# Masked decays on ScalarE for wide float32r products, and group-norm steps on VectorE, in the two mixers of a diffusion block

## Chip, cores and metric

One core of a Trainium2 chip runs the whole program. The metric is device time in microseconds, the median of several executions; lower is better. Engine names are those of the profile: PE (TensorE), PEld (its weight loads), DVE (VectorE), ACT (ScalarE), POOL (GpSimd), SP (SyncE, which issues most DMAs).

## What is computed

Two layers, each of them FFN, mixer, FFN, on 512 latent and 256 context tokens of width 1024, all in float32. The mixer projects the tokens and runs four groups of 256 channels side by side: windowed attention, a bidirectional state-space scan (SSD), grouped-query attention and neighbourhood attention. Each group's output is normalised by its root mean square, and one output projection merges the four. The change touches the SSD group:

```python
def ssd_chunked(x, dt, A, Bh, Ch, h0):
    ...
    cum = jnp.cumsum(dtc * A, axis=2)
    seg = cum[:, :, :, None, :] - cum[:, :, None, :, :]
    lmat = jnp.exp(jnp.where(tril, seg, -jnp.inf))
    att = jnp.einsum('bcihn,bcjhn->bcijh', Cc, Bc) * lmat * dtc[:, :, None]
    y = jnp.einsum('bcijh,bcjhp->bcihp', att, xc)
    ...
    y = y + jnp.einsum('bcihn,bchpn,bcih->bcihp', Cc, jnp.moveaxis(h_start, 0, 1), jnp.exp(cum))
```

The chunk is 128 tokens, there are four heads and two directions, and the last line of `merge_groups` that matters here is `yf * lax.rsqrt(jnp.mean(yf * yf, -1, keepdims=True) + EPS)`, times a gain, per group.

## The kernel before

**Products.** Wide products use float32r: each operand is split into a rounded high part (a cast by ACT, for weights L328) and a low rest (a subtraction by DVE, L329), and `mm3` (L335 to L337) issues three matmuls, high by high, high by low and low by high. Other matmuls have plain float32 operands; the trace shows each of those as two instructions (16 rows for 8 matmuls at L1299).

**Order.** A scheduler orders each engine's instructions when the program is built, from the order in which the code emits them. The mixer interleaves generators: `side_by_side(self.ssd(...), n, projections, 10)` runs the SSD scan beside the projections for the windowed and the grouped-query attention, whose matmuls fill PE while the scan waits for ACT and DVE. Within an engine, instructions run strictly in the order so fixed.

**The scan.** `ssd` makes `dtA` (time step times decay rate, 128 positions by 6 chunks by 8, that is two directions of four heads), then the chunk states, and then calls `chunk_out(t)` per chunk of 128 tokens: chunks 4, 5 (context) and 0 to 3 in layer 0, chunks 0 to 3 in layer 1, ten in all. Per chunk:

- POOL writes two tiles `ld0` and `ld1` of 128x512 (L1294): dtA, spread along the free axis, times the strict triangle GT or LT, for four heads. Each has one buffer, so the next chunk's tiles wait for this chunk's readers.
- PE makes the segment sums `seg` (L1299): per head and direction one 128x128 product with ld as the stationary operand and the triangle U or L as the moving one, eight in all; ACT takes their exponential (`segE`, L1301).
- PE multiplies B by C (`G`, L1304), DVE masks the result (`gm`, L1310) and multiplies it by segE in place and into `att` (L1312), and PE adds up `yd` from both (L1319).
- For the carried state PE makes the cumulative decay in `two[:, 0]` (L1330): per direction, pair and head one 128x128 product, with dtA spread over 64 columns as the stationary operand; and the state's product in `two[:, 1]` (L1332). ACT takes the exponential (`ec`, L1336), and DVE combines all into `zs`.

Chunks 4 and 5 have one direction in the last step, the others two.

**The group norm.** `finish_ssd` calls `group_chunk` for two halves of the channels: ACT squares, POOL multiplies by the gain (L1160), PE sums. `end_group` has DVE compute the reciprocal root, POOL spread it on a diagonal (L1175), PE broadcast it and DVE scale. `place_group` splits the result for the output projection: ACT casts (L1188), POOL subtracts (L1189). These steps run beside the windowed attention.

Other POOL work in the mixers, which stays there: the rotary tables of the grouped-query projections (L862, L866) and the issue of the neighbourhood bias loads (L978 to L981).

Of the kernel before, what the change touches and what calls it, by code (L numbers as in the profile page):

```python
# [11 lines left out]
F32 = mybir.dt.float32  # L12
F32R = mybir.dt.float32r
I32 = mybir.dt.int32
AF = mybir.ActivationFunctionType
ALU = mybir.AluOpType
# [3 lines left out]
P = 128  # L20
# [71 lines left out]
def bcast(ap, n):  # L92

    s = list(ap.shape)
    return ap.unsqueeze(len(s)).to_broadcast(s + [n])


def bcast1(ap, n):

    s = list(ap.shape)  # L100
    return ap.unsqueeze(1).to_broadcast([s[0], n] + s[1:])
# [27 lines left out]
class Block:  # L129
# [1023 lines left out]
    def group_chunk(self, l, group, i, o, y, last, tmp):  # L1153

        nc = self.nc
        nt = 4 if last else 6
        n = nt * P
        sq = self.sb(tmp, [NT], "P", bufs=3)[:, :n]
        nc.scalar.square(sq, o[:, :n])
        nc.gpsimd.tensor_scalar(y[:, i, :n], o[:, :n], self.normT[:, l, 2 * group + i:2 * group + i + 1], None,  # L1160
                                op0=ALU.mult)
        ps = self.ps1()
        for t in range(nt):
            nc.tensor.matmul(ps[:, t:t + 1], lhsT=sq[:, t * P:(t + 1) * P], rhs=self.ones[:, 0:1], start=True, stop=True)
        nc.vector.tensor_copy(self.gss[:, 6 * i:6 * i + nt], ps[:, :nt])

    def end_group(self, y, last, tmp):

        nc = self.nc
        nt = 4 if last else 6  # L1170
        ss = self.sb(tmp, [6], "mss", bufs=2)[:, :nt]
        nc.vector.tensor_tensor(ss, self.gss[:, :nt], self.gss[:, 6:6 + nt], op=ALU.add)
        r = self.rsqrt(tmp, ss, nt, 1.0 / 256)
        dg = self.sb(tmp, [NT], "P", bufs=3).rearrange("p (t c) -> p t c", c=P)[:, :nt]
        nc.gpsimd.tensor_tensor(dg, bcast1(self.ident, nt), bcast(r, P), op=ALU.mult)  # L1175
        for lo, hi in ((0, NX), (NX, NT))[:1 if last else 2]:
            ps = self.ps1()[:, :hi - lo]
            nc.tensor.matmul(ps, lhsT=self.ones, rhs=dg[:, lo // P:hi // P].rearrange("p t c -> p (t c)"),
                             start=True, stop=True)
            for i in range(2):  # L1180
                nc.vector.tensor_tensor(y[:, i, lo:hi], y[:, i, lo:hi], ps, op=ALU.mult)

    def place_group(self, group, y, last):

        n = NX if last else NT
        for i in range(2):
            h, lo = self.act[0][:, 2 * group + i, :n], self.act[1][:, 2 * group + i, :n]
            self.nc.scalar.copy(h, y[:, i, :n])  # L1188
            self.nc.gpsimd.tensor_tensor(lo, y[:, i, :n], h.bitcast(F32), op=ALU.subtract)  # L1189


    def softplus(self, x, tmp):
# [19 lines left out]
    def ssd(self, l, last, tmp):  # L1212
        nc = self.nc
        U, L, GT, LT = (self.cst[:, k:k + P] for k in (K_U, K_L, K_GT, K_LT))
# [3 lines left out]
        self.softplus(dtf, tmp)  # L1218
        dtA = self.sb(tmp, [6, 8], "dtA")
        nc.vector.tensor_tensor(dtA, dt, bcast1(self.A[:, l], 6), op=ALU.mult)  # L1220
        ps = self.ps1()
        for d, m in ((0, GT), (1, LT)):
            nc.tensor.matmul(ps[:, 24 * d:24 * d + 24].rearrange("p (t e) -> p t e", t=6), lhsT=m,
                             rhs=dtA[:, :, 4 * d:4 * d + 4], start=True, stop=True)
# [55 lines left out]
        for t in (3, 2, 1):  # L1280
            v = lambda x: x[:, 1].rearrange("p (h c) -> p h c", h=4)
            x = self.sb(tmp, [256], "ychunk")
            nc.vector.tensor_tensor(x.rearrange("p (h c) -> p h c", h=4), v(state[t]), bcast(dec[:, t, 4:8], 64),
                                    op=ALU.mult)
            nc.vector.tensor_tensor(state[t - 1][:, 1], state[t - 1][:, 1], x, op=ALU.add)

        def chunk_out(t):
            q = col(t)
            first = {4: (1,), 5: (0,)}.get(t, (0, 1))

            ld = []
            for d, m in ((0, GT), (1, LT)):
                x = self.sb(tmp, [4, P], f"ld{d}", bufs=1)
                nc.gpsimd.tensor_tensor(x, bcast(dtA[:, t, 4 * d:4 * d + 4], P), bcast1(m, 4), op=ALU.mult)  # L1294
                ld.append(x)
            seg = self.ps1()
            for h in range(4):
                for d, m in ((0, U), (1, L)):
                    nc.tensor.matmul(seg[:, h * P:(h + 1) * P], lhsT=ld[d][:, h], rhs=m, start=d == 0, stop=d == 1)  # L1299
            E = self.sb(tmp, [2, 2, P], "segE", bufs=1)  # L1300
            nc.scalar.activation(E.rearrange("p g r c -> p (g r c)"), seg, AF.Exp)  # L1301
            G = self.ps1()
            for g in range(2):
                nc.tensor.matmul(G[:, g * P:(g + 1) * P], lhsT=uT[:, 2 + g, q:q + P], rhs=uT[:, 4 + g, q:q + P],  # L1304
                                 start=True, stop=True)
# [10 lines left out]
            for pr in range(2):  # L1316
                for d in range(2):
                    for a in range(2):
                        nc.tensor.matmul(yd[64 * a:64 * a + 64, pr * P:(pr + 1) * P], lhsT=xd[:, d, 2 * pr + a],  # L1319
                                         rhs=att[d][:, pr, a], start=d == 0, stop=d == 1)  # L1320

            two = self.ps2()
            for d, m in ((0, U), (1, L)):
                if d not in first:
                    continue
                for pr in range(2):
                    at = (2 * d + pr) * P
                    for a in range(2):
                        e = 4 * d + 2 * pr + a
                        nc.tensor.matmul(two[64 * a:64 * a + 64, 0, at:at + P],  # L1330
                                         lhsT=dtA[:, t, e:e + 1].to_broadcast([P, 64]), rhs=m, start=True, stop=True)
                    nc.tensor.matmul(two[:, 1, at:at + P], lhsT=state[t][:, d, pr * P:(pr + 1) * P],  # L1332
                                     rhs=uT[:, 4 + pr, q:q + P], start=True, stop=True)
            lo, hi = 256 * first[0], 256 * first[-1] + 256
# [224 lines left out]
```

## Time and profile before

| What | Value |
| --- | --- |
| Median of 3 runs | 2965.39 us (2965.01 to 2967.98) |
| Profiled execution, its own time | 2970.67 us |
| Span in its trace | 2968.9 us |
| Mean granted PE clock | 0.988 of 2.4 GHz |
| Scan and its projections, layer 0 | about 655 to 820 us, chunk outputs from 715 |
| Scan and its projections, layer 1 | about 2250 to 2372 us, chunk outputs from 2305 |
| Windowed attention with the group norm | about 820 to 895 us and 2372 to 2430 us |

The page names what is busy; what counts is what PE waits for in each stage, since an engine that is off the path may idle or work without cost. In the timeline a matmul's start-to-start distance is its price: the durations beside it contain the pipeline's length and overlap.

### The profile page before, as it was taken

What the parts mean: (1) busy time and instruction counts of PE and PEld (TensorE: products, weight loads), DVE (VectorE), ACT (ScalarE), POOL (GpSimd) and SP (SyncE); (2) the same over time, 40 slices, a digit from 0 to 9 for tenths busy, and PEclk for the clock granted to TensorE, in tenths of its full rate; (3) what the DMA queues carried; (4) which work ended last, traced back from release to release, by engine and by line L of the source; (5) the groups of instructions that cost most, each with busy time, mean ns of one, the idle gap of its engine ahead of it and who ended that gap; (6) DMA issues with size and microseconds to landing.
All of it is one profiled execution on the core that took longest, in us unless ns stands there. A gap on an engine that the chain in (4) does not pass through costs nothing.

```text
span 2968.9 us, 43652 instructions
## 1 busy us (share of the span) xinstructions
PE 2867.3 (97%) x16412; PEld 2451.8 (83%) x16412; DVE 2068.6 (70%) x4258; ACT 1149.6 (39%) x2103; POOL 494.2 (17%) x372
## 2 busy tenths in 40 slices
PE   7999999999999998999999999999999999899997
PEld 4898888888787777888878789999988787788886
DVE  4766668775758787666577976766886757776558
ACT  4333233352256543322324433333344256443333
POOL 1222122100110002221211122221200110012112
PEclk9999999999999999999999999999999999999998
DMA  6443334231124223534435122212132143242332
GB/s 230 144 162 107 121 100 141 77 100 49 29 78 83 94 72 104 178 122 141 157 103 168 57 67 75 76 58 74 56 97 72 44 110 89 78 125 86 95 100 72
DMA packets 319207, 296.09 MB, mean 100 GB/s; under 512 B 16311, under 2 KB 244751, under 8 KB 318739
## 3 DMA queue, kind: packets, MB, share of 16 engines
q1 hardware_dynamic: 317939, 290.80, 31.6%
q0 software_dynamic: 1056, 2.49, 0.4%
q8 instruction: 130, 2.13, 0.3%
q14 instruction: 82, 0.67, 0.1%
HBM read 270.52 MB, written 7.39 MB: 94 GB/s over the span
## 4 chain that ended last, share of the span: by engine, by line
PE 77%; DVE 15%; issue 3%; ACT 2%; DMA 2%; POOL 0%; SPq 0%; DVEq 0%; ACTq 0%; POOLq 0%
PE ps L335 12%; PE ps L337 12%; PE ps L336 12%; PE psp L335 9%; PE psp L337 9%; PE psp L336 9%; PE ps L260 2%; PE ps L1033 2%; DVE wl L329 2%; PE ps L1075 2%; DVE tmp L472 2%; PE psp L1091 2%; DVE res L465 2%; DVE res L474 1%; DVE actl L392 1%
## 5 line engine op out<-in xcount | busy, mean ns | idle before, releaser
L328 ACT CAST wh<-wraw 128x512 fp32r<-128x512 f32 x570 | 352.1, 621 | 873.2 <-PE ps L337 457.2
L329 DVE TENSOR_TENSOR wl<-wraw,wh 128x512 fp32r<-128x512 f32 x570 | 416.0, 736 | 330.4 <-ACT wh L328 324.2
L335 PE MATMUL psp<-acth,wh 128*128 128x384 f32 (+2 forms) x1432 | 482.9, 338 | 4.5 <-DVE e L701 1.9
L336 PE MATMUL psp<-actl,wh 128*128 128x384 f32 (+2 forms) x1432 | 481.0, 336 | 5.1 <-DVE actl L392 4.9
L337 PE MATMUL psp<-acth,wl 128*128 128x384 f32 (+2 forms) x1432 | 478.6, 335 | 4.6 <-DVE wl L329 4.6
L335 PEld LDWEIGHTS psp<-acth,wh 128*128 128x128 f32 x1432 | 271.6, 190 | 44.7 <-issue 27.3
L328 ACT CAST wh<-wrax 128x512 fp32r<-128x512 f32 x280 | 173.9, 622 | 339.9 <-PE ps L336 201.6
L336 PEld LDWEIGHTS psp<-actl,wh 128*128 128x128 f32 x1432 | 271.9, 190 | 20.3 <-DVE actl L392 7.0
L337 PEld LDWEIGHTS psp<-acth,wl 128*128 128x128 f32 x1432 | 272.2, 190 | 16.2 <-DVE wl L329 5.2
L335 PE MATMUL ps<-S,wh 128*128 128x384 f32 (+1 forms) x840 | 276.7, 329 | 7.8 <-DVE e L692 4.8
L336 PE MATMUL ps<-S,wh 128*128 128x384 f32 (+1 forms) x840 | 275.8, 328 | 0.0
L337 PE MATMUL ps<-S,wl 128*128 128x384 f32 (+1 forms) x840 | 275.6, 328 | 0.0
L329 DVE TENSOR_TENSOR wl<-wrax,wh 128x512 fp32r<-128x512 f32 x280 | 212.5, 764 | 84.3 <-ACT wh L328 59.0
L335 PE MATMUL ps<-acth,wh 128*128 128x512 f32 (+2 forms) x688 | 245.7, 358 | 3.2 <-ACT wh L328 1.7
L336 PE MATMUL ps<-actl,wh 128*128 128x512 f32 (+2 forms) x688 | 244.2, 355 | 0.0
L337 PE MATMUL ps<-acth,wl 128*128 128x512 f32 (+2 forms) x688 | 243.3, 354 | 0.0
L335 PE MATMUL ps<-wh,gTh 128*128 128x512 f32 x594 | 235.1, 396 | 7.6 <-DVE tmp L472 7.6
L337 PE MATMUL ps<-wh,gTl 128*128 128x512 f32 x594 | 233.4, 393 | 0.0
L336 PE MATMUL ps<-wl,gTh 128*128 128x512 f32 x594 | 233.4, 393 | 0.0
L474 DVE TENSOR_TENSOR res<-res,tmp 128x512 f32<-128x512 f32 x268 | 188.0, 732 | 0.6
L335 PEld LDWEIGHTS ps<-S,wh 128*128 128x128 f32 x840 | 159.2, 189 | 12.6 <-issue 6.8
L337 PEld LDWEIGHTS ps<-S,wl 128*128 128x128 f32 x840 | 159.3, 190 | 0.0
(376 smaller groups left out, 5470.8 us busy)
## 6 DMA issues: line engine op xcount, KB each, us to landing
araw<-in_ada_w_dram SPq DMA_DIRECT2D x128, 512.0 KB
wraw<-in_ffn_w_out_dram SPq DMA_DIRECT2D x88, 512.0 KB
wrax<-in_ffn_w_in_dram SPq DMA_DIRECT2D x160, 256.0 KB
wraw<-in_ffn_w_in_dram SPq DMA_DIRECT2D x120, 256.0 KB
wraw<-in_mix_w_in_dram SPq DMA_DIRECT2D x44, 512.0 KB
wraw<-in_ffn_w_in_dram SPq DMA_DIRECT2D x36, 512.0 KB
wraw<-in_mix_w_out_dram SPq DMA_DIRECT2D x16, 512.0 KB
mrow<-mrow SPq DMA_DIRECT2D x10, 512.0 KB
```

Source lines behind the costliest of these rows:

```text
L260: nc.tensor.matmul(ps[32 * g:32 * g + 32, :], lhsT=self.cs[:, k, c0:c0 + 32], rhs=w[:, k - kk, :], start=i == 0 and k < 4, stop=i == len(n ...
L328: self.nc.scalar.copy(h, raw)
L329: self.nc.vector.tensor_tensor(lo, raw, h.bitcast(F32), op=ALU.subtract)
L335: mm(out, lhsT=a[0], rhs=b[0], start=start, stop=False)
L336: mm(out, lhsT=a[0], rhs=b[1], start=False, stop=False)
L337: return mm(out, lhsT=a[1], rhs=b[0], start=False, stop=stop)
L465: nc.vector.tensor_tensor(r, r, x[:, lo:hi], op=op)
L472: nc.vector.tensor_tensor(y, acc, mrow[0 if t < 4 else 1][:, dh * 512:(dh + 1) * 512], op=ALU.mult)
L474: nc.vector.tensor_tensor(r, r, y, op=ALU.add)
L1033: nc.tensor.matmul(ps[:, at:at + hi - lo], lhsT=q, rhs=part[:, lo:hi], start=i == 0, stop=i == 1)
L1075: nc.tensor.transpose(pt[:, j * P:(j + 1) * P], p[:, a:a + P], self.ident)
L1091: nc.tensor.matmul(out[64 * a:64 * a + 64, :], lhsT=v[:, kt, vcol:vcol + 64], rhs=pT[:, i], start=i == 0, stop=i == len(order) - 1)
```

## The change

`ssd` splits dtA into a high and a low float32r part, casts GT and LT to float32r, and fills two constant 128x128 tiles (`half0`, `half1`) that have ones in the left or the right 64 columns. In `chunk_out` the triangles U and L, scaled by a head's dtA, become the moving operand: ACT writes sixteen 128x128 pieces (two directions, high and low, four heads) into four tiles ld00, ld01, ld10 and ld11 of 128x512 with one buffer each. The segment sums are then four float32r products of 512 columns with GT or LT as the stationary operand, and the cumulative decay is four float32r products of 256 columns per direction with half0 or half1. The three steps of the group norm that POOL had go to DVE.

```diff
@@ group_chunk, end_group, place_group
-        nc.gpsimd.tensor_scalar(y[:, i, :n], o[:, :n], self.normT[:, l, 2 * group + i:2 * group + i + 1], None,
+        nc.vector.tensor_scalar(y[:, i, :n], o[:, :n], self.normT[:, l, 2 * group + i:2 * group + i + 1], None,
...
-        nc.gpsimd.tensor_tensor(dg, bcast1(self.ident, nt), bcast(r, P), op=ALU.mult)
+        nc.vector.tensor_tensor(dg, bcast1(self.ident, nt), bcast(r, P), op=ALU.mult)
...
-            self.nc.gpsimd.tensor_tensor(lo, y[:, i, :n], h.bitcast(F32), op=ALU.subtract)
+            self.nc.vector.tensor_tensor(lo, y[:, i, :n], h.bitcast(F32), op=ALU.subtract)
@@ ssd, behind dtA
+        parts = [self.sb(tmp, [6, 8], x, F32R) for x in ("dtAh", "dtAl")]
+        nc.scalar.copy(parts[0], dtA)
+        nc.vector.tensor_tensor(parts[1], dtA, parts[0].bitcast(F32), op=ALU.subtract)
+        before = [self.sb(tmp, [P], x, F32R) for x in ("GTr", "LTr")]
+        for x, m in zip(before, (GT, LT)):
+            nc.scalar.copy(x, m)
+        halves = [self.sb(tmp, [P], f"half{a}", F32R) for a in range(2)]
+        for a, x in enumerate(halves):
+            nc.vector.tensor_copy(x, self.zero.to_broadcast([P, P]))
+            nc.vector.tensor_copy(x[:, 64 * a:64 * a + 64], self.ones[:, :64])
@@ chunk_out
-            for d, m in ((0, GT), (1, LT)):
-                x = self.sb(tmp, [4, P], f"ld{d}", bufs=1)
-                nc.gpsimd.tensor_tensor(x, bcast(dtA[:, t, 4 * d:4 * d + 4], P), bcast1(m, 4), op=ALU.mult)
-                ld.append(x)
-            seg = self.ps1()
-            for h in range(4):
-                for d, m in ((0, U), (1, L)):
-                    nc.tensor.matmul(seg[:, h * P:(h + 1) * P], lhsT=ld[d][:, h], rhs=m, start=d == 0, stop=d == 1)
+            for d, m in ((0, U), (1, L)):
+                hi, lo = (self.sb(tmp, [4, P], f"ld{d}{i}", F32R, bufs=1) for i in range(2))
+                ld.append((hi, lo))
+                for x, part in zip((hi, lo), parts):
+                    for h in range(4):
+                        nc.scalar.mul(x[:, h], m, part[:, t, 4 * d + h:4 * d + h + 1].bitcast(F32))
+                for i, x in enumerate((hi, lo)):
+                    nc.tensor.matmul(seg, lhsT=before[d], rhs=x.rearrange("p h c -> p (h c)"), start=d + i == 0,
+                                     stop=d + i == 2)
...
+            for d in first:
+                for i in range(4):
+                    x = ld[d][i // 2].rearrange("p (r a) c -> p a r c", a=2)[:, i % 2]
+                    nc.tensor.matmul(two[:, 0, 256 * d:256 * d + 256].rearrange("p (r c) -> p r c", r=2), lhsT=halves[i % 2],
+                                     rhs=x, start=i == 0, stop=i == 3)
...
-                    for a in range(2):
-                        e = 4 * d + 2 * pr + a
-                        nc.tensor.matmul(two[64 * a:64 * a + 64, 0, at:at + P],
-                                         lhsT=dtA[:, t, e:e + 1].to_broadcast([P, 64]), rhs=m, start=True, stop=True)
```

How the instructions stand now, at two places. First PE at chunk 1 of layer 1. Before (ld0 and ld1 are the two directions' tiles, ps1 holds seg):

```order
L1299 MATMUL ps1_4058_21477<-cst_3868_20380,ld0_4056_21473 128x128
L1299 MATMUL ps1_4058_21477<-cst_3868_20380,ld1_4057_21475 128x128
L1299 MATMUL ps1_4058_21477<-cst_3868_20380,ld0_4056_21473 128x128
L1299 MATMUL ps1_4058_21477<-cst_3868_20380,ld1_4057_21475 128x128
L1299 MATMUL ps1_4058_21477<-cst_3868_20380,ld0_4056_21473 128x128
L1299 MATMUL ps1_4058_21477<-cst_3868_20380,ld1_4057_21475 128x128
L1299 MATMUL ps1_4058_21477<-cst_3868_20380,ld0_4056_21473 128x128
L1299 MATMUL ps1_4058_21477<-cst_3868_20380,ld1_4057_21475 128x128
L1304 MATMUL ps1_4060_21488<-uT_3884_20401 128x128 x2
```

And with the change (line numbers of the changed file; L1312 makes seg, L1318 G, L1340 the cumulative decay, L1345 the state's product, L1333 yd):

```order
L1312 MATMUL ps1_4082_21585<-ld00_4083_21586,GTr_3972_21021 128x512
L1312 MATMUL ps1_4082_21585<-ld01_4084_21587,GTr_3972_21021 128x512
L1312 MATMUL ps1_4082_21585<-ld10_4085_21598,LTr_3973_21022 128x512
L1312 MATMUL ps1_4082_21585<-ld11_4086_21599,LTr_3973_21022 128x512
L1318 MATMUL ps1_4088_21612<-uT_3902_20487 128x128 x2
L1340 MATMUL ps2_4094_21636<-ld00_4083_21586,half0_3974_21025 128x256
L1340 MATMUL ps2_4094_21636<-ld00_4083_21586,half1_3975_21026 128x256
L1340 MATMUL ps2_4094_21636<-ld01_4084_21587,half0_3974_21025 128x256
L1340 MATMUL ps2_4094_21636<-ld01_4084_21587,half1_3975_21026 128x256
L1340 MATMUL ps2_4094_21636<-ld10_4085_21598,half0_3974_21025 128x256
```

Eight plain products became four wide ones, and the tiles ld are now read a second time, by L1340, and so come free later.

Second, ACT in layer 0 from the last but one chunk (2) to the last (3). Before:

```order
L791 COPY cqT_995_5385<-ps2_1234_6914 128x256
L328 CAST wh_1347_7466<-wraw_1346_7464 128x512
L328 CAST wh_1349_7470<-wraw_1346_7464 128x512
L878 ACTIVATE tA_1265_7076<-ps2_1264_7071 128x512
L1301 ACTIVATE segE_1285_7159<-ps1_1284_7150 128x512
L1301 ACTIVATE segE_1298_7220<-ps1_1297_7211 128x512
```

With the change (L1310 are the decays of chunk 3, L1349 is ec of chunk 2, L1315 segE of chunk 3):

```order
L328 CAST wh_1409_7746<-wraw_1406_7740 128x512
L1310 ACTIVATE ld00_1312_7282<-cst_989_5376,dtAh_1076_6032 128x128 x4
L1310 ACTIVATE ld01_1313_7283<-cst_989_5376,dtAl_1077_6033 128x128 x2
L1349 ACTIVATE ec_1309_7272<-ps2_1308_7259 128x512
L1310 ACTIVATE ld01_1313_7283<-cst_989_5376,dtAl_1077_6033 128x128 x2
L1310 ACTIVATE ld10_1314_7294<-cst_989_5376,dtAh_1076_6032 128x128 x4
L791 COPY ckT_996_5386<-ps2_1287_7170 128x256
L1310 ACTIVATE ld11_1315_7295<-cst_989_5376,dtAl_1077_6033 128x128 x4
L1315 ACTIVATE segE_1316_7306<-ps1_1311_7281 128x512
```

Before, the exponentials of chunks 2 and 3 stood next to each other; now sixteen multiplications stand between chunk 2's products and chunk 3's exponential, with ec and a copy among them.

## Rows read from the trace of the kernel before

**Rows 1.** The page, part 1: busy time, share of the span, instructions by engine.
```profile
PE 2867.3 (97%) x16412; PEld 2451.8 (83%) x16412; DVE 2068.6 (70%) x4258; ACT 1149.6 (39%) x2103; POOL 494.2 (17%) x372
```

**Rows 2.** Waits of PE over the whole span: us in total, times, longest us.
```profile
PE ps L1319 <- DVE att L1312: 6.6, 5, 1.7
```

**Rows 3.** Windows of the mixers' stages: length, busy by engine (instructions), PEclk, DMA, GB/s.
```profile
715.00:820.00 105.00, 99.53 (x660) 78.05 (x659) 74.20 (x211) 23.90 (x44) 15.42 (x15) 0.95 0.11 30
820.00:895.00 75.00, 73.47 (x523) 62.15 (x523) 40.52 (x120) 41.08 (x99) 10.24 (x5) 1.00 0.35 89
2310.00:2372.00 62.00, 58.70 (x405) 46.27 (x404) 45.63 (x130) 14.88 (x27) 10.08 (x11) 1.00 0.15 42
2372.00:2430.00 58.00, 58.00 (x395) 49.29 (x393) 28.31 (x84) 31.95 (x69) 6.71 (x5) 1.00 0.32 86
```

**Rows 4.** Timeline of PE, a wait of layer 0: start, us, instruction, [idle before].
```profile
774.02 0.40 PE L335 MATMUL psp<-acth,wh 128*128 128x512 f32 x1
775.94 0.43 PE L1319 MATMUL ps<-att,xw 128*64 128x128 f32 x2 [1.53 <-DVE att L1312]
```

**Rows 5.** Timeline of POOL in the same place.
```profile
772.27 2.04 POOL L1294 TENSOR_TENSOR ld<-dtA,cst 128x512 f32<-128x512 f32 x2 [19.10 <-PE ps L1299]
```

**Rows 6.** Timeline of DVE there, and the same line again 13 us later.
```profile
772.37 0.97 DVE L399 TENSOR_SCALAR rs<-rs 128x8 int32<-128x8 int32 x1
773.37 0.97 DVE L400 TENSOR_SCALAR rs<-rs 128x8 int32<-128x8 int32 x1
...
785.41 0.17 DVE L399 TENSOR_SCALAR rs<-rs 128x4 int32<-128x4 int32 x1
```

**Rows 7.** Windows behind two such waits, columns as in rows 3.
```profile
757.00:761.00 4.00, 4.00 (x18) 2.57 (x18) 1.46 (x5) 0.00 (x0) 0.00 (x0) 0.59 0.01 2
776.00:786.00 10.00, 10.00 (x38) 6.90 (x39) 6.87 (x19) 0.50 (x2) 2.84 (x3) 0.66 0.01 2
```

**Rows 8.** Timeline of PE, chunk 1 of layer 1.
```profile
2320.70 1.95 PE L1299 MATMUL ps<-cst,ld 128*128 128x128 f32 x16
2322.49 0.61 PE L1304 MATMUL ps<-uT 128*128 128x128 f32 x4
2323.03 0.44 PE L1330 MATMUL ps<-cst,dtA 128*64 128x128 f32 x4
2323.40 0.49 PE L1332 MATMUL ps<-uT,st 128*128 128x128 f32 x2
```

**Rows 9.** Timeline of PE, float32r products of 512 and of 256 columns.
```profile
656.66 0.39 PE L335 MATMUL psp<-acth,wh 128*128 128x512 f32 x1
656.89 0.39 PE L336 MATMUL psp<-actl,wh 128*128 128x512 f32 x1
...
661.10 0.28 PE L335 MATMUL psp<-acth,wh 128*128 128x256 f32 x1
661.22 0.28 PE L336 MATMUL psp<-actl,wh 128*128 128x256 f32 x1
```

**Rows 10.** ACT groups by shape: busy us, mean ns of one, idle before.
```profile
L1099 ACT COPY oT<-psp 128x128 f32<-128x128 f32 x40 | 10.6, 265 | 15.8 <-PE psp L1091 15.2
L949 ACT COPY pcol<-ps 128x256 f32<-128x256 f32 x7 | 2.7, 381 | 0.0
L1145 ACT ACTIVATE acth<-ps,smT 128x256 fp32r<-128x256 f32 x6 | 2.7, 474 | 2.3 <-PE ps L1142 2.3
L1009 ACT CAST aQ<-aqT 128x256 fp32r<-128x256 f32 x10 | 3.7, 403 | 0.0
```

**Rows 11.** Timeline of ACT, three casts of 128x256 back to back.
```profile
820.49 1.02 ACT L1009 CAST aQ<-aqT 128x256 fp32r<-128x256 f32 x3
```

**Rows 12.** DVE groups by shape, 545 to 1090 us.
```profile
L1133 DVE TENSOR_SCALAR yf<-yf,rs 128x256 f32<-128x256 f32 x12 | 3.3, 348 | 0.1
L647 DVE TENSOR_TENSOR gTl<-ffg,gTh 128x768 fp32r<-128x768 f32 x2 | 1.9, 954 | 0.0
```

**Rows 13.** Timeline of PE, a wait beside the group norm's last step in layer 0.
```profile
892.05 0.44 PE L783 MATMUL psp<-ident,pcol 128*128 128x128 f32 x2 [0.99 <-DVE pcol L906]
```

More of the change, by code (lines that the diff above doesn't have):

```diff
@@ L1289, in chunk_out @@
             first = {4: (1,), 5: (0,)}.get(t, (0, 1))
+            seg = self.ps1()
             ld = []
-            for d, m in ((0, GT), (1, LT)):
-                x = self.sb(tmp, [4, P], f"ld{d}", bufs=1)
-                nc.gpsimd.tensor_tensor(x, bcast(dtA[:, t, 4 * d:4 * d + 4], P), bcast1(m, 4), op=ALU.mult)
-                ld.append(x)
-            seg = self.ps1()
-            for h in range(4):
-                for d, m in ((0, U), (1, L)):
-                    nc.tensor.matmul(seg[:, h * P:(h + 1) * P], lhsT=ld[d][:, h], rhs=m, start=d == 0, stop=d == 1)
+            for d, m in ((0, U), (1, L)):
[7 more added lines that the diff above has]
+                                     stop=d + i == 2)
             E = self.sb(tmp, [2, 2, P], "segE", bufs=1)
@@ L1322, in chunk_out @@
             two = self.ps2()
-            for d, m in ((0, U), (1, L)):
-                if d not in first:
-                    continue
+            for d in first:
[3 more added lines that the diff above has]
+                                     rhs=x, start=i == 0, stop=i == 3)
+            for d in first:
                 for pr in range(2):
                     at = (2 * d + pr) * P
-                    for a in range(2):
-                        e = 4 * d + 2 * pr + a
-                        nc.tensor.matmul(two[64 * a:64 * a + 64, 0, at:at + P],
-                                         lhsT=dtA[:, t, e:e + 1].to_broadcast([P, 64]), rhs=m, start=True, stop=True)
                     nc.tensor.matmul(two[:, 1, at:at + P], lhsT=state[t][:, d, pr * P:(pr + 1) * P],
```

## Prediction

> **What bounds the kernel now.** I read the busy shares first: PE is busy for 97% of the span, DVE for 70%, ACT for 39%, POOL for 17% [rows 1]. PE is the bound, so the time changes by what PE's own work changes and by what PE waits for. Next come the windows of the two mixers' scan and of the attention behind each [rows 3]: in layer 0's chunk outputs PE is idle for 105 - 99.5 = 5.5 us and the granted clock is 0.95; in layer 1's it is idle for 3.3 us at full clock; in the attention with the group norm it is idle for 1.5 us and for nothing. ACT is busy for a quarter of the scan windows, DVE for some 70%.
>
> The list of PE's waits names the scan's: `yd` for `att`, five times, 6.6 us in all, 1.7 at most [rows 2]. One of them shows the cause: PE issues a projection at 774.02 and the next product only at 775.94, having waited 1.53 us for DVE's att [rows 4]. DVE was not short of time: two steps of a reciprocal root on 8 columns took 0.97 us each, where the same line takes 0.17 a little later [rows 6], and exactly then, from 772.27 for 2.04 us, POOL made the next chunk's ld tiles [rows 5]. So POOL's tiles hold DVE up by 2 x 0.8 = 1.6 us, and PE pays it where it has nothing else in front.
>
> **The change, part by part.** *PE's work.* Prices are start-to-start distances. The sixteen instructions of the segment sums last from 2320.70 to 2322.49, 1.79 us, 0.11 each; four instructions of the cumulative decay take 2323.40 - 2323.03 = 0.37 us, so sixteen take 1.48 [rows 8]. In their place come four float32r products of 512 columns at 0.23 us and eight of 256 columns at 0.12 us, priced by the projections, which also load new weights for each [rows 9]: 0.91 and 0.96 us. That saves 0.88 + 0.52 = 1.40 us in each of eight chunks with both directions, 11.2 us. Chunks 4 and 5 have half of the decay products: 0.88 + (0.74 - 0.48) = 1.14 us each, 2.3 us. Together **-13.5 us**, all on PE's own queue. Bounds: -13.5 with the rows' pitch; if the strided 256-column operand ran at half the rate, 72 products would cost 0.12 more each, 8.6 us, leaving -4.9.
>
> *The waits for att.* The ten POOL pairs are gone, so each of the five waits ends up to 1.6 us sooner. The longest keeps about 0.1. I take **-6.5** of 6.6; the other bound is 0, if something else is late in their place.
>
> The Trainium skill ("SBUF — State Buffer", section "SBUF: two separate sides") says that DVE and GpSimd share a port pair as an exclusive lock, so that the one that comes second stands still for the other's whole instruction. The trace agrees here with 0.97 against 0.17 us. By the rule the lock does not matter how small the DVE instruction is, and taking POOL out frees DVE entirely; by the rows alone I can only claim the places where a stretch was seen, and the sum above uses those.
>
> *The clock.* Behind two of these waits the granted clock is 0.59 for 4 us and 0.66 for 10 us [rows 7]: that work would need 4 x 0.41 + 10 x 0.34 = 5.0 us less at full clock. With the waits gone the cause that stands in front of them is gone. But waits of like length in layer 1 are followed by a full clock [rows 3], so it is not certain that each execution pays it; I take **-3**, between -5 and 0.
>
> *ACT's new work.* Sixteen multiplications of 128x128 per chunk, 160 in all. No such row exists. A copy of 128x128 takes 265 ns; a per-partition scale adds 474 - 381 = 93 ns; a source in SBUF 403 - 381 = 22 [rows 10]: 380 ns busy. Three casts of 128x256 back to back take 1.02 us, not 1.21, so each follows the other after 0.31 us, 0.09 below its duration [rows 11]: 0.29 us per multiplication, 4.6 us per chunk, 46 us in all. ACT has room for it in total: 24 us of 105 are used [rows 3], and 28 come on top. What counts is the order. The four ld tiles have one buffer each and are now read until the cumulative-decay products, so the next chunk's burst can begin only there. Where the next segment sums come many projections later (chunks 4, 5, 0 of layer 0, and 0 to 2 of layer 1) the burst is hidden by them. It is not at four places. Worked through for chunk 3 of layer 0, from the start of chunk 2's decay products: these take 0.96 us, the state's products 8 x 0.11 = 0.86, the first segment product 0.23. ACT begins at 0.3, does six multiplications to 2.1, ec to 2.65 and two more to 3.2. The second segment product waits from 2.05 to 3.3, that is 1.2 us. The third finds its tile ready. The last reader of ld11 has to wait for a copy and eight more multiplications, until 6.0 in place of 5.1: 0.9 us. Then att needs segE, and yd waits another 0.8. That is 2.9 us; by the same count chunk 2 loses 0.9, chunk 1 0.35, layer 1's chunk 3 0.3, and some 0.5 comes on top where the first projection behind the scan waits for its accumulators. **+5**. Bounds: 0, and four whole bursts, +18.5.
>
> The wait that is added on ACT's queue stands ahead of weight casts and accumulator copies. The casts are several projections ahead of their use, and the copies come before the next but one accumulator is wanted; their cover is the same projections, and without it they would add the lateness just counted, not another one.
>
> *The group norm.* DVE takes over two scalings, one diagonal and two subtractions per layer. A 128x768 two-input operation takes 0.95 us; a scaling of 256 columns takes 0.35 [rows 12], so 768 take under 0.95 as well: below 5 x 0.95 = 4.8 us in layer 0 and two thirds of it in layer 1, 8 us. DVE is busy for 40.5 us of 75 and 28.3 of 58 there, and PE is idle for 1.5 and 0 [rows 3], so it hides; without that cover it would cost up to +8. On the other side PE waits 0.99 us at 892.05 for a DVE copy [rows 13] behind a subtraction that POOL's L1189 had stretched; about half of that should go. **-0.5**.
>
> *The setup.* Two casts, a split of 48 columns and four small fills per layer lie beside projections that keep PE fed: 0, and 2 us at most if all were on the path. No DMA is added or moved; POOL's queue only gets shorter.
>
> **The sum.** -13.5 - 6.5 - 3 + 5 - 0.5 = -18.5 us, made against the profiled execution (2970.67 us, 5.3 above the median of the runs): 2952 for such an execution, and 2965.4 - 18.5 = **2947 us** for the median.
>
> **The rivals.** *The scan loses its waits entirely.* The scheduler's order hides the bursts, the clock stays full: -13.5 - 6.6 - 5 - 1 = -26, 2939 us. For it: ACT's total room. Against it: the count of chunk 3. Chance 0.2.
>
> *ACT takes POOL's place as the late one.* The waits for att go, but about as much comes back as waits for seg, +10 in place of +5, and the clock drops as before: -13.5 - 6.5 + 10 + 5 = -5, 2960 us. For it: in-order ACT with tiles of one buffer. Chance 0.11.
>
> *The wide products are not as cheap as the projections.* Were the 256-column ones at half rate, the sum is -18.5 + 8.6 = -10, 2955 us; were the 512-column ones as well, 40 x 0.23 = 9.2 more, and the time is 2965 less 1: the change would not do what it says. Against both: the same shapes at 0.12 and 0.23 [rows 9]. Chance 0.06, mostly on the faster side.
>
> *Slower: small ACT instructions carry the scan.* Were each multiplication to cost its full 0.38 us plus a wait of its own, 0.47 in all as in the longest row of that width [rows 10], a chunk needs 7.5 us of ACT. The scan turns slower where a chunk's lateness exceeds 23.5 us / 10 = 2.35 us. The shortest cover is about 4.3 us (decay, state and half a projection); 7.5 - 4.3 = 3.2 us in every chunk gives +32 against -23.5: 2974 us. For it: ACT's in-order queue. Against it: in six chunks of ten the cover is a whole projection. Chance 0.05.
>
> The Trainium skill ("ScalarE: Activation LUTs", section "What ACT_TABLE_LOAD costs") speaks against cutting ACT's work up so small: it gives an ACTIVATE 186 ns plus 0.833 per element, 93 more per pointer operand, and 93 of overlap back to back, an estimate of 386 ns busy and 293 apart for 128 columns, of which only 107 are work. The rows give 380 and 290, so the sum by the rule is the same, and the rival stays at its price.
>
> **How the numbers follow.** The forecast itself (2942 to 2954) has 0.58, and the rest is as told. A measurement of this kernel can tell about 0.2%, 6 us, from no change. Faster by more than that: the forecast, the full gain and most of the dear products, 0.84. Within it: ACT's lateness and the worst of the dear products, 0.11. Slower: 0.05. The range runs from a little below the full gain to ACT's lateness, 2936 to 2960.
>
> **What would show it.** In the profile after: PE has 304 instructions of L1299 and L1330 fewer and 112 new ones; PE is busy for some 13 us less; POOL for 39 less; ACT for about 60 more, in 160 rows near 0.38 us. No DVE step of 8 columns takes 0.97 us in the scan. The wait of yd for att shrinks to under 2 us, and waits of segment or decay products for ACT's ld show up, the longest at layer 0's chunk 3. The granted clock of layer 0's chunk outputs rises from 0.95. The prediction is wrong if L1312 is not 0.23 us apart, if PE waits for ld by more than 10 us, or if the clock falls in new places.

## Result and profile after

| Kernel | Median (range) | Against the kernel before, 95% interval |
| --- | --- | --- |
| before | 2966.26 us (2965.01 to 2967.98) | |
| changed | 2945.31 us (2939.89 to 2951.31) | 0.9929 [0.9909, 0.995] |

The changed kernel is faster by 21 us; the forecast was 2947 in 2936 to 2960. Its profiled execution took 2945.09 us, with a span of 2943.3 and a granted clock of 0.991.

The page's part 1 of the changed kernel answers to [rows 1]:

```profile
PE 2844.5 (97%) x16220; PEld 2437.0 (83%) x16220; DVE 2062.5 (70%) x4278; ACT 1196.5 (41%) x2269; POOL 460.5 (16%) x342
```

PE is busy for 22.8 us less (some 13 were foretold), with the 192 instructions fewer that were foretold, POOL for 33.7 less (39) and ACT for 46.9 more (about 60). The new ACT rows (group: busy, mean ns of one, idle before) are as priced; 160 of them about 0.295 apart make 47 us, since overlapped instructions count once in busy time:

```profile
L1310 ACT ACTIVATE ld<-cst,dtAh 128x128 fp32r<-128x128 f32 x80 | 26.4, 395 | 3.2 <-PE ps L1340 1.8 <-PE ps L1312 1.1
L1310 ACT ACTIVATE ld<-cst,dtAl 128x128 fp32r<-128x128 f32 x80 | 26.4, 392 | 0.0
```

PE's waits over the span, those of the scan and its end, answer to [rows 2]:

```profile
PE psp L335 <- DVE dqT L906: 2.4, 1, 2.4
...
PE ps L1312 <- ACT ld L1310: 1.1, 1, 1.1
...
PE psp L335 <- ACT dqT L903: 1.0, 1, 1.0
...
PE ps L1340 <- ACT ld L1310: 0.3, 1, 0.3
...
PE ps L1333 <- DVE att L1326: 0.2, 1, 0.2
```

The five waits for att, 6.6 us, are down to one of 0.2. In their place PE waits 1.4 us for ACT's ld, at chunk 3 of layer 0 as counted, and 2.4 + 1.0 us behind the two scans for dqT, the queries of the neighbourhood attention, whose copies free the accumulators. Before, it waited for dqT in layer 0 alone:

```profile
PE psp L335 <- DVE dqT L906: 0.9, 1, 0.9
```

The windows of layer 0's chunk outputs and of the attention behind them, as [rows 3]:

```profile
715.00:803.00 88.00, 84.18 (x542) 68.08 (x541) 66.18 (x205) 45.91 (x123) 4.42 (x5) 1.00 0.15 42
803.00:875.00 72.00, 70.66 (x493) 59.61 (x494) 36.53 (x118) 37.84 (x92) 0.00 (x0) 0.98 0.27 69
```

The chunk outputs run at full clock now (0.95 before); PE's loss now stands in the first microseconds of the next stage. The timeline there, PE, ACT and DVE together, shows how:

```profile
795.65 0.50 PE L1312 MATMUL ps<-ld,GTr 128*128 128x512 f32 x1 [1.15 <-ACT ld L1310]
...
800.40 0.59 ACT L903 ACTIVATE dqT<-psp 128x512 f32<-128x512 f32 x1
...
802.84 0.61 DVE L1357 SCALAR_TENSOR_TENSOR ychunk<-uT,Dp,ychunk 128x128 f32<-128x128 f32 x2
...
803.49 0.42 DVE L1360 TENSOR_TENSOR zs<-zs,ychunk 128x256 f32<-128x256 f32 x1
803.83 0.41 DVE L906 TENSOR_SCALAR dqT<-psp 128x256 f32<-128x256 f32 x1
...
804.30 0.79 PE L335 MATMUL psp<-acth,wh 128*128 128x512 f32 x1 [2.41 <-DVE dqT L906]
```

The projections beside the scan are used up before its last chunk ends. DVE's copy L906, which frees the accumulator for the next projection, stands behind the chunk's last output steps (L1357, L1360) on DVE's queue, and nothing covers PE meanwhile.

**A sharper measure.** Both mixers are compared below by their length in the profile, from the first transpose of a `pcol` tile (L783) to the last of L1142. Outside the mixers the profiled spans come to between 2384 and 2393 us in all kernels, without a pattern. Layer 1's mixer has a granted clock of 1.00 in all of them; layer 0's has 0.97 in the profile of before, 0.98 in e4's, 0.99 in e1's, e5's, e12's and the changed kernel's first, and 1.00 in e3's, e7's and e9's. A hundredth of it is some 3 us of that mixer, so small differences in layer 0 can be clock.

| Kernel | Mixer, layer 0 | Mixer, layer 1 | Both |
| --- | --- | --- | --- |
| before | 324.7 | 255.8 | 580.5 |
| e1, norm only | 318.9 | 256.0 | 574.9 |
| e3, no POOL tiles, plain products | 313.5 | 253.3 | 566.8 |
| e4, POOL tiles, wide products | 316.1 | 251.7 | 567.8 |
| e5, wide segments, plain decays | 312.5 | 250.8 | 563.3 |
| e12, the same, decays grouped | 307.0 | 247.3 | 554.3 |
| changed, e9 (again) | 307.7, 306.4 | 248.1, 248.2 | 555.8, 554.6 |
| e7, copy on ScalarE | 303.3 | 248.0 | 551.3 |

The busy time of each engine in the two mixers together, for e1 and then for e9:

```profile
sum 574.90, PE 556.83 PEld 447.29 DVE 393.01 ACT 276.01 POOL 34.15; mean PE 278.41 PEld 223.65 DVE 196.51 ACT 138.00 POOL 17.07
```

```profile
sum 554.60, PE 538.95 PEld 436.40 DVE 383.31 ACT 312.84 POOL 16.93; mean PE 269.48 PEld 218.20 DVE 191.65 ACT 156.42 POOL 8.46
```

### The profile page after: what moved, and what is told of

The parts are those of the page before. It is cut to its first block, busy times and chain, and to the rows that moved or that the text cites. A ratio compares the mean times of both kernels' runs of the same rounds, so it can differ in the third digit from the quotient of the medians.

```text
span 2943.3 us, 43403 instructions
## 1 busy us (share of the span) xinstructions
PE 2844.5 (97%) x16220; PEld 2437.0 (83%) x16220; DVE 2062.5 (70%) x4278; ACT 1196.5 (41%) x2269; POOL 460.5 (16%) x342
## 4 chain that ended last, share of the span: by engine, by line
PE 78%; DVE 14%; issue 3%; ACT 2%; DMA 2%; POOL 0%; SPq 0%; DVEq 0%; ACTq 0%; POOLq 0%
PE ps L335 12%; PE ps L337 12%; PE ps L336 12%; PE psp L335 9%; PE psp L337 9%; PE psp L336 9%; PE ps L260 2%; PE ps L1033 2%; PE ps L1075 2%; PE psp L1091 2%; DVE wl L329 2%; DVE tmp L472 2%; DVE res L465 2%; DVE res L474 1%; DVE actl L392 1%
## 5 line engine op out<-in xcount | busy, mean ns | idle before, releaser
L335 PEld LDWEIGHTS ps<-S,wh 128*128 128x128 f32 x840 | 158.7, 189 | 12.9 <-issue 6.9
L336 PEld LDWEIGHTS ps<-S,wh 128*128 128x128 f32 x840 | 158.7, 189 | 0.0
## 6 DMA issues: line engine op xcount, KB each, us to landing
wrax<-in_ffn_w_in_dram SPq DMA_DIRECT2D x160, 256.0 KB
wraw<-in_ffn_w_in_dram SPq DMA_DIRECT2D x120, 256.0 KB
```

The source lines that it names most:

```text
L335: mm(out, lhsT=a[0], rhs=b[0], start=start, stop=False)
L336: mm(out, lhsT=a[0], rhs=b[1], start=False, stop=False)
```

## Experiments

**e1 and e2: the two halves of the change.** e1 is the kernel before with this alone, and e2 the changed kernel with it undone:

```diff
-        nc.gpsimd.tensor_scalar(y[:, i, :n], o[:, :n], self.normT[:, l, 2 * group + i:2 * group + i + 1], None,
+        nc.vector.tensor_scalar(y[:, i, :n], o[:, :n], self.normT[:, l, 2 * group + i:2 * group + i + 1], None,
...
-        nc.gpsimd.tensor_tensor(dg, bcast1(self.ident, nt), bcast(r, P), op=ALU.mult)
+        nc.vector.tensor_tensor(dg, bcast1(self.ident, nt), bcast(r, P), op=ALU.mult)
...
-            self.nc.gpsimd.tensor_tensor(lo, y[:, i, :n], h.bitcast(F32), op=ALU.subtract)
+            self.nc.vector.tensor_tensor(lo, y[:, i, :n], h.bitcast(F32), op=ALU.subtract)
```

> The kernel before, with only the group norm's scaling, diagonal and subtraction on VectorE. My theory: hidden work; the wait of 0.99 us for pcol behind the norm's subtraction goes, the decays' waits for att (6.6 us) stay: 0 to -1.5 us against the kernel before. Rival (VectorE pays for it): up to +8 us. Rival (a good part of the gain comes from the group norm, through GpSimd leaving the shared port): -4 us or more.

> The changed kernel with the group norm's three steps back on GpSimd. My theory: all but 0 to 1.5 us of the gain stays, so 18 to 21 us below the kernel before, PE busy for 22 us less and a wait of about 1 us for pcol back in the group norm. Rival (the group norm carries a good part): 16 us or less below.

e1: 2966.64 us, 0.9998 [0.9989, 1.0007]. e2: 2946.24 us, 0.9931 [0.9918, 0.9943]. The group norm is worth nothing that can be measured (e1's interval reaches from 3 us faster to 2 us slower), though its wait of 1.0 us for pcol [rows 13] goes in e1 and comes back in e2. Among e1's waits of PE, the one for att is as before:

```profile
PE ps L1319 <- DVE att L1312: 6.6, 5, 1.7
```

e1 also bears on the clock. Its chunk outputs of layer 0, with the same waits, ran at 0.98 and not 0.95 (the last but two of these numbers):

```profile
723.70:830.60 106.90, 100.90 (x661) 79.43 (x661) 70.09 (x201) 23.96 (x45) 12.78 (x13) 0.98 0.17 46
```

Its mixers took 5.6 us less than in the profile of before, which is 5.3 above its own median. In the ten microseconds behind its wait of 1.53 us for att, at 775 us, the clock was 1.00, where the profile of before has 0.66 [rows 7]. So a low clock does not follow these waits every time.

**e3 and e4: the port or the products.** e3 takes the kernel before and leaves its products alone:

```diff
-                nc.gpsimd.tensor_tensor(x, bcast(dtA[:, t, 4 * d:4 * d + 4], P), bcast1(m, 4), op=ALU.mult)
+                for h in range(4):
+                    nc.scalar.mul(x[:, h], m, dtA[:, t, 4 * d + h:4 * d + h + 1])
```

> The kernel before with its two decay tiles per chunk made by eight ScalarE multiplications instead of two GpSimd operations; products, their number and GpSimd's group norm unchanged. My theory (GpSimd's tiles hold VectorE up and PE pays): the waits for att fall from 6.6 to under 1 us, the granted clock of layer 0's chunk outputs rises from 0.95, and the time is 6 to 10 us below the kernel before. Rival (only the cheaper products count, the waits move elsewhere): within 2 us of the kernel before.

e4 takes the changed kernel and gives POOL two operations per chunk again:

```diff
-                for x, part in zip((hi, lo), parts):
-                    for h in range(4):
-                        nc.scalar.mul(x[:, h], m, part[:, t, 4 * d + h:4 * d + h + 1].bitcast(F32))
+                nc.gpsimd.tensor_tensor(hi, bcast(parts[0][:, t, 4 * d:4 * d + 4].bitcast(F32), P), bcast1(m, 4), op=ALU.mult)
+                for h in range(4):
+                    nc.scalar.mul(lo[:, h], m, parts[1][:, t, 4 * d + h:4 * d + h + 1].bitcast(F32))
```

> The changed kernel with the two hi tiles of each chunk made by GpSimd, in the shape that the kernel before has (one 128x512 operation each), ScalarE makes the lo tiles only; the wide products stay. My theory: VectorE's small steps stretch to about 1 us again, waits for att or for ld of 4 to 7 us come back, and the time is 9 to 14 us below the kernel before (7 to 12 above the changed kernel). Rival (only the cheaper products count): as the changed kernel, 20 us below. Rival (ScalarE's sixteen multiplications cost something, so halving them gains): 21 us or more below.

e3: 2955.40 us, 0.9958 [0.9945, 0.997], a gain of 11.4, a little over the 6 to 10 that I expected, though its interval reaches down to 9. e4: 2955.24 us, 0.9959 [0.9945, 0.9973], a gain of 11.5. Each half alone gives about half of the changed kernel's gain, so both causes are real and none of these rivals stands. In e3 both scans have a full clock, and of the waits for att one is left:

```profile
PE ps L1320 <- DVE att L1313: 0.2, 1, 0.2
```

In e4 POOL and DVE stand in the timeline like this, at layer 0's last chunk:

```profile
796.96 0.17 DVE L400 TENSOR_SCALAR rs<-rs 128x4 int32<-128x4 int32 x1
797.11 2.04 POOL L1308 TENSOR_TENSOR ld<-dtAh,cst 128x512 fp32r<-128x512 f32 x2 [0.54 <-PE ps L1340]
797.17 1.00 DVE L402 TENSOR_TENSOR rs<-rs 128x4 f32<-128x4 f32 x1
...
798.20 0.96 DVE L403 SCALAR_TENSOR_TENSOR rs<-rs,rs 128x4 f32<-128x4 f32 x1
...
799.20 0.16 DVE L404 SCALAR_TENSOR_TENSOR rs<-rs,rs 128x4 f32<-128x4 f32 x1
```

Two DVE steps on four columns take 1.00 and 0.96 us, exactly while POOL's two operations last, and the next takes 0.16: the stretch of [rows 5, 6], moved to other steps. PE's waits for DVE are back with it, for att and segE (3.9 us) and, more, for tB, a tile of the grouped-query projections (5.0 us, 0.2 in the changed kernel):

```profile
PE ps L790 <- DVE tB L887: 5.0, 3, 1.8
PE ps L1333 <- DVE att L1326: 2.6, 5, 1.2
...
PE ps L1333 <- DVE segE L1326: 1.3, 1, 1.3
```

One of these steps on eight columns, in layer 0's chunk outputs (group: busy, mean ns, idle), fell in the changed kernel from a mean of 718 ns to this:

```profile
L400 DVE TENSOR_SCALAR rs<-rs 128x8 int32<-128x8 int32 x3 | 0.5, 160 | 0.0
```

**e5: only the segment sums wide.** The cumulative decays are as in the kernel before:

```diff
+            for d, m in ((0, U), (1, L)):
+                if d not in first:
+                    continue
-            for d in first:
-                for i in range(4):
-                    x = ld[d][i // 2].rearrange("p (r a) c -> p a r c", a=2)[:, i % 2]
-                    nc.tensor.matmul(two[:, 0, 256 * d:256 * d + 256].rearrange("p (r c) -> p r c", r=2), lhsT=halves[i % 2],
-                                     rhs=x, start=i == 0, stop=i == 3)
-            for d in first:
                 for pr in range(2):
                     at = (2 * d + pr) * P
+                    for a in range(2):
+                        e = 4 * d + 2 * pr + a
+                        nc.tensor.matmul(two[64 * a:64 * a + 64, 0, at:at + P],
+                                         lhsT=dtA[:, t, e:e + 1].to_broadcast([P, 64]), rhs=m, start=True, stop=True)
                     nc.tensor.matmul(two[:, 1, at:at + P], lhsT=state[t][:, d, pr * P:(pr + 1) * P],
                                      rhs=uT[:, 4 + pr, q:q + P], start=True, stop=True)
```

> The changed kernel with the cumulative decays again as sixteen plain products of 128 columns with the decay column broadcast as weights; the segment sums stay wide. My theory: PE's own work rises by 8 x 0.52 + 2 x 0.26 = 4.7 us, the ld tiles come free earlier so that the waits for ACT's ld (1.1 and 0.3 us in the changed kernel) vanish, and the time is 16 to 19 us below the kernel before. Rival (the eight 256-column products with strided operands cost as much as what they replace, or their hold on the ld tiles costs it back): as the changed kernel or faster, 20 us or more below.

2951.34 us, 0.995 [0.9937, 0.9964]: only 14.1 below the kernel before. Waits for ld are gone as expected, but in layer 0 as much came up at the scan's end, where the wait for dqT is now 3.8 us in place of 1.4 + 2.4:

```profile
PE psp L335 <- DVE dqT L906: 3.8, 1, 3.8
```

So what ends late there is DVE, with or without waits for ACT. From e3, where this wait is 0.9 us, to e5 the mixers gain only 566.8 - 563.3 = 3.5 us. And the products cost more than I had priced. The timeline of PE in layer 1, against the changed kernel's, shows where. e5:

```profile
2307.68 0.61 PE L1318 MATMUL ps<-uT 128*128 128x128 f32 x4
2308.21 0.44 PE L1344 MATMUL ps<-cst,dtA 128*64 128x128 f32 x4
2308.58 0.49 PE L1346 MATMUL ps<-uT,st 128*128 128x128 f32 x2
2309.00 0.44 PE L1344 MATMUL ps<-cst,dtA 128*64 128x128 f32 x4
2309.37 0.49 PE L1346 MATMUL ps<-uT,st 128*128 128x128 f32 x2
```

Changed:

```profile
2300.85 0.70 PE L1312 MATMUL ps<-ld,GTr 128*128 128x512 f32 x2
2301.39 0.63 PE L1312 MATMUL ps<-ld,LTr 128*128 128x512 f32 x2
2301.86 0.61 PE L1318 MATMUL ps<-uT 128*128 128x128 f32 x4
2302.22 1.19 PE L1340 MATMUL ps<-ld,half 128*128 128x256 f32 x8
2303.25 0.83 PE L1345 MATMUL ps<-uT,st 128*128 128x128 f32 x6
...
2306.11 0.39 PE L1333 MATMUL ps<-att,xw 128*64 128x128 f32 x4
2306.33 0.39 PE L1333 MATMUL ps<-segE,xw 128*64 128x128 f32 x4
```

Where products of 64 and of 128 columns of the array alternate (128*64 and 128*128 in the rows), four narrow ones take 0.37 us from start to start and two wide ones 0.42, 0.79 per round. In runs of their own kind four narrow ones take 0.22 (2306.33 - 2306.11), and two wide ones 0.22, at 0.11 each. So a round loses 0.35 us to its two changes, 0.15 and 0.20. Likewise the four products of L1318 take 0.53 ahead of narrow ones and 0.36 ahead of wide ones. The Trainium skill ("TensorEngine Tiling (Array Packing)", section "Key Properties") says that changing the tiling mode drains TensorE; these rows agree, in that each change costs time here. The accumulator is not the cause: L1318's four are followed by products into another accumulator in both cases.

**e12: the same, grouped.** To tell the width of the decay products from the order that the change brought along, e12 is e5 with one loop made into two:

```diff
                         nc.tensor.matmul(two[64 * a:64 * a + 64, 0, at:at + P],
                                          lhsT=dtA[:, t, e:e + 1].to_broadcast([P, 64]), rhs=m, start=True, stop=True)
+            for d in first:
+                for pr in range(2):
+                    at = (2 * d + pr) * P
                     nc.tensor.matmul(two[:, 1, at:at + P], lhsT=state[t][:, d, pr * P:(pr + 1) * P],
                                      rhs=uT[:, 4 + pr, q:q + P], start=True, stop=True)
```

> The kernel of e5 (cumulative decays as plain products) with one loop made into two, so that a chunk's decay products (64 columns of the array each) all stand ahead of its state products (128 columns), as the changed kernel has it, instead of alternating four and two. My theory from e5's and the first trace: four decay products take 0.22 us in a run but 0.37 between others, and two state products 0.42 instead of 0.22, so each change between the two widths costs about 0.2 us; a chunk's decays and states then take about 2.1 us instead of 3.15, as in the changed kernel (1.9), and the time is 5 to 7 us below e5, 19 to 22 below the kernel before. Then the wide decay products themselves gain next to nothing, and the loops' order what they were priced at. Rival (plain products of 128 columns are dear by themselves, at 0.09 us each as priced): 14 to 16 us below the kernel before, like e5.

2942.61 us, 0.9921 [0.9906, 0.9937]: 8.7 us below e5, more than the 5 to 7 expected, and not to be told from the changed kernel. Its PE timeline at the same place of layer 1:

```profile
2298.01 0.60 PE L1318 MATMUL ps<-uT 128*128 128x128 f32 x4
2298.55 1.09 PE L1344 MATMUL ps<-cst,dtA 128*64 128x128 f32 x16
2299.57 0.94 PE L1349 MATMUL ps<-uT,st 128*128 128x128 f32 x6
```

Sixteen plain decay products in a row take 1.02 us; the changed kernel's eight wide ones take 1.03. By the code, three rounds fewer in eight chunks and one fewer in two make 26 x 0.35 = 9.1 us. Counted in the timelines of the mixers, where the scheduler puts other products between, there are 50 changes of width fewer, 25 rounds, 8.8 us; the mixers differ by 563.3 - 554.3 = 9.0. In layer 1, at full clock in both, it is 10 rounds, 3.5 us, and 250.8 - 247.3 = 3.5. In time the wide decay products gain nothing over grouped plain ones.

**e6 and e7: the waits that came in place.** e6 gives the ld tiles of the first direction a second buffer; e7 moves the copy that PE waited for:

```diff
-                hi, lo = (self.sb(tmp, [4, P], f"ld{d}{i}", F32R, bufs=1) for i in range(2))
+                hi, lo = (self.sb(tmp, [4, P], f"ld{d}{i}", F32R, bufs=2 - d) for i in range(2))
```

> The changed kernel with two buffers instead of one for the two ld tiles of the first direction (there is no room for more). My theory: the waits of L1312 and L1340 for ACT's ld (1.1 and 0.3 us at layer 0's chunk 3) fall to under 0.5 us together; as that chunk is followed by a wait of 2.4 us for dqT, part of it comes back there: 0 to -3 us against the changed kernel, 20 to 23 below the kernel before. Rival (ACT's burst is not limited by the buffers): the same waits, 20.5 below.

```diff
-                nc.vector.tensor_scalar(d[:, NX:], pc[:, :NCTX], scale, None, op0=ALU.mult)
+                nc.scalar.mul(d[:, NX:], pc[:, :NCTX], scale)
```

> The changed kernel with the attention inputs' context columns copied from PSUM by ScalarE instead of VectorE (L906; six small copies per layer, at most). My theory: PE's wait of 2.4 us for dqT behind layer 0's scan exists because the copy stands behind chunk 3's five output steps on VectorE; on ScalarE it ends about 801, before the projections need the accumulators, so that this wait falls below 0.5 us and the clock of the 10 us behind it stays full: 2 to 4 us below the changed kernel, 22 to 25 below the kernel before. Rival (the last projection's end is what PE waits for, or ScalarE then delays something else): within 1 us of the changed kernel.

e6: 2944.23 us, 0.9933 [0.9921, 0.9946], no different from the changed kernel. Its waits of PE in the scan:

```profile
PE ps L1333 <- DVE segE L1326: 1.2, 1, 1.2
...
PE ps L1340 <- DVE ec L1350: 0.8, 1, 0.8
...
PE ps L1312 <- ACT ld L1310: 0.2, 1, 0.2
```

ACT's 1.4 us became 0.2, and 2.0 us of waits for DVE came up at the same place, at 795 and 800 us: DVE was as late as ACT there. So the single buffer shows in the list but does not set the time.

e7: 2941.01 us, 0.9915 [0.9901, 0.9928]. The copy ends in time, and PE goes on without a wait:

```profile
800.41 0.39 ACT L906 ACTIVATE dqT<-psp 128x256 f32<-128x256 f32 x1
...
801.35 0.50 PE L335 MATMUL psp<-acth,wh 128*128 128x512 f32 x1
```

**e8: the tiles on VectorE.** One operation of 128x512 per tile takes the place of four multiplications:

```diff
-                    for h in range(4):
-                        nc.scalar.mul(x[:, h], m, part[:, t, 4 * d + h:4 * d + h + 1].bitcast(F32))
+                    nc.vector.tensor_tensor(x, bcast(part[:, t, 4 * d:4 * d + 4].bitcast(F32), P), bcast1(m, 4), op=ALU.mult)
```

> The changed kernel with the four decay tiles of each chunk made by VectorE, one 128x512 operation each, instead of by sixteen ScalarE multiplications. My theory: 40 operations of about 0.7 us add 28 us to an engine that is busy for 70 to 76 percent of the scan; its steps come before att, so waits for att or for ld return at 2 us in half of the chunks: 8 to 16 us above the changed kernel, 4 to 12 below the kernel before. Rival (VectorE is fast enough with GpSimd off its port, and ScalarE's queue is relieved): 20 us or more below the kernel before.

2950.20 us, 0.995 [0.9937, 0.9962]: 5 to 7 us above the changed kernel (2945.31 and, in e9, 2943.36), less than I expected. The forty operations take 0.68 us each as foreseen; waits for att and segE come to only 1.2 us (0.2 in the changed kernel), and it is the waits for the projections' tC (a tile of the rotary step) that grow, from 1.5 to 4.5 us:

```profile
PE ps L790 <- DVE tC L803: 4.5, 3, 2.4
```

**e9 to e11: side by side.** The changed kernel, e7's, and e7 with e6's buffers, in one comparison:

> The changed kernel itself, once more beside the next two, so that they are compared on one chip. Both theories: 20 to 22 us below the kernel before, waits as in its first profile (2.4 us for dqT, 1.1 and 0.3 us for ld behind layer 0's scan).

> The kernel of e7 once more. My theory (the wait of 2.4 us and the half clock behind it are real and gone): 3 to 5 us below the changed kernel of this call, 23 to 26 below the kernel before. Rival (e7 was a lucky set of runs): within 1.5 us of the changed kernel.

> e7 and e6 together: the context copy on ScalarE and two buffers for the first direction's ld tiles. My theory from e6 (where the waits for ld went, waits for segE and ec took their place, since VectorE's steps of the last chunks are then the late ones): 0 to 1 us below e7's kernel of this call. Rival (behind the shorter end of the scan the 1.4 us of ld waits are gained in full): 1.5 to 3 us below it.

| Kernel | Median (range) | Against before |
| --- | --- | --- |
| e9, changed | 2943.36 us (2940.28 to 2949.00) | 0.9928 [0.9914, 0.9942] |
| e10, copy on ScalarE | 2941.27 us (2938.22 to 2942.16) | 0.9914 [0.9901, 0.9927] |
| e11, and two buffers | 2940.99 us (2937.75 to 2946.57) | 0.9916 [0.9904, 0.9929] |

The copy's gain is smaller than the 3 to 5 us I gave it: 2.1 us here, some 4 between e7 and the first runs of the changed kernel, and 2.9 to 4.4 in the length of layer 0's mixer, taking both profiles of each kernel. The intervals overlap, so by times alone it is likely and not certain. The two buffers add nothing on top.

e9 also bears on the clock. It has the same wait for dqT as the changed kernel's first profile:

```profile
803.65 0.50 PE L335 MATMUL psp<-acth,wh 128*128 128x512 f32 x1 [2.42 <-DVE dqT L906]
```

The windows behind it are, for that first profile and then for e9:

```profile
805.00:807.00 2.00, 2.00 (x6) 1.54 (x5) 0.98 (x3) 0.24 (x1) 0.00 (x0) 0.50 0.70 158
804.00:814.00 10.00, 9.70 (x48) 8.38 (x49) 2.51 (x5) 2.46 (x6) 0.00 (x0) 0.84 0.67 157
```

```profile
804.00:814.00 10.00, 10.00 (x57) 8.75 (x56) 3.48 (x7) 2.43 (x5) 0.00 (x0) 1.00 0.67 157
```

Half the clock for some microseconds in one execution, all of it in the other, behind the same work; in e2, with the same wait, it is 1.00 too. What decides it is not shown. Such a wait can cost 10 x 0.16 = 1.6 us more than its length, but need not.

## Why the prediction was right, and where it was not

The direction and the size were right, and so were two mechanisms: POOL's hold on DVE and the cheaper segment sums. The decays' gain had another cause and was about twice as large, ACT's cost was right in sum and came mostly at another place, and the clock was read from one execution. That the sum came within 4 us owes something to luck: PE's work was priced 3.3 us too low (-13.5 against 7.8 + 9.0) and the clock 1 to 3 us too high.

- **PE's work, -13.5.** PE's busy time in the mixers is 16.7 to 17.9 us below e1's (540.1 and 539.0 against 556.8), of which up to 2 are e1's clock. In layer 1, at full clock, it is 6.4 to 6.6 against the 5.6 that I priced for four chunks. The parts differ more than their sum. The segment sums save 1.79 - 1.01 = 0.78 us in the chunk shown and not 0.88 (0.25 apart on average, the last two 0.47 / 2 = 0.23). The decays' saving of 0.52 per chunk is the step that failed: from [rows 8] I took four instructions at 0.37 us for sixteen at 1.48, and did not read on to the next row, where two state products need 0.42. Two fifths of the 0.37 were the change of width. What gained, 9 us in all from e5 to e12, was that the two widths no longer alternate, which I had priced at nothing. e12 gets this from the state products' loop of their own. The changed kernel has that loop too, but its decay products use 128 columns like the state products, so it would have no change of width between them in either order; wide decays in one loop with the state products were not run. Beyond that the float32r form of the decays gained no time over grouped plain products.
- **The waits for att, -6.5.** Confirmed: 6.6 us became 0.2, e3 puts it at 8.1 us of mixer time against e1 (of which up to 2 are again e1's clock), and e4 brings back the stretched steps, waits of 3.9 us for att and segE and 5.0 for tB. That POOL's tiles were the cause is shown by e3 and e4 together.
- **The clock, -3.** Too much certainty in one execution. The low clock that I read [rows 7] was in the profiled execution; e1 has the same waits and 0.98. Against the median this term is between 0 and about 2 us, an estimate whose upper end is from e1's 106.9 us at 0.98. That the bounds reached to 0 was right. A clock that falls in a new place, one of my signs of being wrong, did show in the changed kernel's first profile (0.50 behind the wait for dqT), and not in e9's.
- **ACT's new work, +5.** The price of a multiplication was right (0.39 against 0.38 busy, 0.295 against 0.29 apart), and chunk 3's first wait was 1.1 us against 1.2 counted. The other waits of that count (0.9, 0.8, 0.9, 0.35, 0.3) are 0.3 and 0.2 or absent. But the end of the scan, which I gave +0.5, took 2.4 - 0.9 = 1.5 us in layer 0 and 1.0 in layer 1. It made 1.4 + 1.5 + 1.0 = 3.9 us in place of 5, mostly at another place. What ended late there was DVE's copy in layer 0 and in layer 1 ACT's own copies of dqT (L903), but not a burst: e8, with no such multiplications on ACT, has the same 1.0 us in layer 1. That the sum came out near 5 is luck.
- **The group norm, -0.5, and the setup, 0.** Nothing measurable (e1, and e2 against the changed kernel), as priced.

The measured parts, 10 x 0.78 for the segments, 9.0 for the end of the alternation and 6.4 for the waits, less 3.9 for the new ones, make 19.3; the mixers show 574.9 - 554.6 = 20.3, and the medians of the changed kernel 20.9 and 22.1. The rival with ACT as the late one is refuted by the result, and e6 says why: with most of ACT's waits taken away the time stayed, since DVE was as late. That rival's sum also has a slip: a clock that drops as before adds nothing to the time before, so without its last +5 it is -10, 2955 us.

The fastest kernels run were e7 (e10) and e11, at 0.9914 to 0.9916, and e12 is near with 0.9921. e12 still has a wait of 3.8 us for dqT, which e7's edit might take away; the two together were not run, nor was the kernel before with its loop split alone.

## What to carry to other kernels

When a matmul is priced from a timeline, look at what stands on both sides of it: here it paid to issue products that use 64 columns of the array and products that use 128 in runs, and two loops in place of one (e12) gave as much as a new form of the products. When one engine's small steps take a second engine's operation length, move the second engine's work, and expect the gain only where PE has nothing else in front. After removing a wait, look at the end of the stage: what covered PE there may now be used up earlier, and the next late thing may be a small copy that stands behind a chain on an in-order queue.

## What the hardware showed that I had not expected

A change between 64-column and 128-column products cost 0.15 to 0.20 us, more than a plain product of 128 columns (0.11). In a run, plain 64-column products followed each other after 0.06 us on average (16 in 1.02), so that sixteen took as long as the eight float32r products of 256 columns that replace them (1.03). And the granted clock behind one and the same wait of 2.4 us was 0.50 in one execution and 1.00 in another.
